# An encoder layer's expert stage: look-up order, early list rows, an early row tile and rested buffers

## The chip, the cores and the metric

The kernel runs on one core of a Trainium2 chip. The metric is the device time of one execution in microseconds (us); lower is better. The engines of the core are named as the profile names them: PE (matrix multiply, with PEld for its weight loads), DVE (vector), ACT (scalar), POOL (GpSimd, which also issues the indirect DMAs) and SP (which only issues DMAs). Each engine takes its instructions in the order in which the program put them into its queue, and an instruction that waits holds everything behind it on the same engine.

## The reference

One layer of an encoder over 256 tokens of width 2048: a retention and recurrent block, cross attention, and then PEER, a layer of 16384 single-neuron experts, ended by a normalisation. The change touches only PEER and the glue before it:

```python
def peer_ffn(xn, w_q, sub_keys, u_tab, v_tab):
    q = (xt @ w_q).reshape(t, PEER_HEADS, 2, PEER_HALF)
    sub_scores = jnp.einsum('thcd,hckd->thck', q, sub_keys)
    vals, ids = lax.top_k(sub_scores, PEER_TOPK)
    ...
    eid = (i1 * PEER_N_KEYS + i2)          # 8 heads x 16 experts a token
    gate = softmax(top_sc)
    ...
        u = u_tab[eb]
        act = gelu(einsum('td,tkd->tk', xb, u))
        return einsum('tk,tkd->td', gb * act, v_tab[eb])
```

Every token picks 128 experts. An expert costs a dot product of the token's normed row with a row of `u_tab` and the addition of a multiple of a row of `v_tab`; a row is 2048 floats, 8 KB.

## The kernel before

The kernel doesn't gather all chosen rows. It treats the experts in three ways.

- **Dense.** `RD` = 40 groups of 128 experts are computed for all tokens as matrix products: five chunks (0 to 4) of eight columns, with weights that SP loads in order (`U`, `V`).
- **Counted.** Among the other 88 groups, the 32 experts of each lane that most tokens chose are found on the chip (`choose`, `chosen_rows`) and also computed for all tokens: four chunks (5 to 8) of eight columns, whose rows are gathered by POOL with indices in `dyn`.
- **Listed.** What remains is a list for each token, `BASE` = 38 places. Tokens are lanes, in two halves `tt` of 128 tokens; place `k` of half `tt` is one gather by POOL of 128 rows (1 MB) with indices `idx[tt][:, k]`, then one DVE instruction: `dot` with a row of `Us`, later `axpy` with a row of `Vs`. The few tokens with longer lists share two `spill` operations, each with two gathers (rows of `Us`, and normed rows from `hn` in device memory).

The stages around the change, in order of time:

**The look-ups.** While PE does the last columns of the dense U chunks (`u_block`), a generator `side` is woven in: after each half column `Weave.pump` lets as much of it run as its rate allows. Before it, `gbuild` writes the gate of each expert and token to device memory (`gt<-gs`, issued by ACT); its source tiles come from the slots `qs` and `ms`, three of them in `ms`. `look_up` then finds for each token which of its experts are counted. It has eight parts, four for each half; part `i` needs one 1 MB tile of broadcast indices, loaded by `at_load(i)` on POOL into `ats[i % 6]`. The list `ats` is `h[1]`, the three `ms` tiles, and two tiles that `gbuild` uses for scratch (`gx["a"]`, `gx["d"]`). After the four parts of a half, `compact` picks its list (`pick`, `rows_of`), and after both halves it works out the spills; then the three `ms` tiles go to `ring`, the free list for gathered list rows. In this part of the program a scheduler orders the instructions; the stages after it (`manual_schedule`) are issued as written.

**The D steps.** `run` goes through a list of steps with the loads, splits and matmuls of each. A loop over `t` does, at step `t`: the transposes of step `t + 4` (`turned`), the high part of step `t + 3` on ACT (`high`), the low part of step `t + 2` on DVE (`low`), the loads for step `t + 8` (or `t + 12` for gathered rows of V and of gates), the matmuls of step `t`, and then `wv.pump(step.rate)`, which lets the generator `chosen` do list operations; one costs 2.2. The 64 D steps are the U products of the counted chunks 5 to 8, two steps to a gathered row. `chosen` refills every free buffer of `ring` with the next gather before each operation. The first half's dots use the normed rows in `h[0]`; after the last of them `hold(1)` loads the second half's rows over it, on POOL. The two spills stand between the halves.

**The V steps.** `ORDER` is the order of the chunks: 0, 1, 2, 3 (dense, 16 W steps each), then 5, 6, 7, 8 (counted, 16 R steps each), and 4 in `v_final`. Chunks 5 and 7 are `PLAIN`: their R steps run in plain float32 without a split. A counted chunk first needs its gates: a K step multiplies by 1 MB of gate rows that POOL gathers in eight parts, one at a step (`pending`). Rows of gates and of V go to the free list `rows_v`. A buffer returns to it as soon as its last reader has been issued (in `low`, or after the matmuls of a plain step). The list starts empty: when a chunk's activations are no longer needed, `given(n)` hands their tile over, to `rows_v` for `n` below 6 and to `ring` after that. The tile of chunk 0 is lent to the dense weights as two halves (`lent`) and goes to `rows_v` when the queue of W and G loads (`queues["WG"]`; G steps read dense gates) is empty.

**The end.** `v_final` does chunk 4, the last `END` = 12 axpys, the spills' second part and the final norm.

Of the kernel before, what the change touches and what calls it, by code (L numbers as in the profile page):

```python
# [18 lines left out]
P = 128  # L19
# [15 lines left out]
ND = 2  # L35
RL, RT, RN = 1.55, 2.6, 1.4
RQ = 1.3
RG, RK, RU, RV, RP = 8.0, 3.5, 2.05, 1.2, 2.0
PLAIN = (4, 5, 7)
END = 12  # L40
WARM = 18
RD = 40
RS = P - RD
# [42 lines left out]
def hybrid_layer_kernel(ctx: ExitStack, tc: tile.TileContext, a: dict, out: bass.AP, dbg=None):  # L86
# [23 lines left out]
    def slot(tag, shape, name, dt=F32):  # L110
        return b8.tile(shape, dt, tag=tag, name=name, bufs=3 if tag == "ms" else 2)
# [878 lines left out]
    def look_up(tt):  # L990
        fl = gx["b"][:, 1920:2048]
        for c in range(4):
            at = at_of(4 * tt + c)
            for n in range(0, 32, 16):
                V.tensor_scalar(at[:, n:n + 16], at[:, n:n + 16], tr["t"][:, P:], None, op0=ALU.is_equal)
                yield 0.7
            pt = sm("look")
            for n in range(32):
                PE.matmul(pt[:, NW * n:NW * n + NW], at[:, n], words, start=True, stop=True)
            if 4 * tt + c + len(ats) < 4 * TT:  # L1000
                at_load(4 * tt + c + len(ats))
            found = gx["b"][:, 512:512 + 32 * NW].rearrange("p (s w) -> p s w", w=NW)
            V.tensor_tensor(found, pt[:, :32 * NW].rearrange("p (s w) -> p s w", w=NW),
                            which[tt][:, 32 * c:32 * c + 32], op=ALU.mult)
            V.tensor_reduce(fl[:, 32 * c:32 * c + 32], found, axis=AX.X, op=ALU.add)
            yield 1.0
        fu = fl.bitcast(U32)
        V.tensor_copy(fl.bitcast(I32), fl)
        V.tensor_tensor(fu, fu, bits[tt], op=ALU.logical_shift_right)
        V.tensor_scalar(fu, fu, 31, None, op0=ALU.logical_shift_left)  # L1010
        for t in (key[tt], work[tt]):
            V.tensor_tensor(t.bitcast(U32), t.bitcast(U32), fu, op=ALU.bitwise_or)
        yield 1.0

    def compact():
        ct = pgt.tile([P, 5, TT], F32, tag="ct", name="ct")
        cnt_, more, off, end, tok = (ct[:, n] for n in range(5))
        for tt in range(TT):
            yield from look_up(tt)
            if not tt:  # L1020
                yield from chosen_rows()
            sel[tt] = tp.tile([P, NSEL], F32, tag=f"sel{tt}", name="sel")
            sel2[tt] = tp.tile([P, NSEL], F32, tag=f"gts{tt}", name="sel2")
            idx[tt] = tp.tile([P, NSEL], I32, tag=f"idx{tt}", name="idx")
            for b in range(NSEL // 8):
                pick(tt, b)
                yield 0.8
            m8 = pgt.tile([P, OVK], F32, tag="m8", name="m8")
            V.max(m8[:, :8], key[tt])
            V.tensor_scalar(more[:, tt:tt + 1], m8[:, :1], 0.0, None, op0=ALU.is_ge)  # L1030
            V.tensor_scalar(m8[:, :OVK], sel[tt][:, BASE:], 0.0, None, op0=ALU.is_ge)
            V.tensor_reduce(cnt_[:, tt:tt + 1], m8[:, :OVK], axis=AX.X, op=ALU.add)
            V.tensor_scalar(tok[:, tt:tt + 1], tr["t"][:, P:], float(tt * P), None, op0=ALU.add)
            for n, t in enumerate((key[tt], work[tt])):
                A.dma_start(spare_keys[tt, n], t)
            rows_of(tt, slice(0, NSEL))
            ov[tt] = pgt.tile([P, OVK], F32, tag=f"ov{tt}", name="ov")
            V.tensor_copy(ov[tt], idx[tt][:, BASE:])
            yield 1.4
# [44 lines left out]
                                   op0=ALU.is_equal, op1=ALU.mult, accum_out=spl["g"][:, bs])  # L1084
            yield 0.6
        count_rest()
        ring.extend(ats[1:4])

    tr = {}

    def side():
        tr["t"] = rp.tile([P, P + 1], F32, tag="cand", name="tri")
        nc.sync.dma_start(tr["t"], a["tri"])
        wv.rate = RK
        ats.extend(slot("ms", [P, D], f"at{i}") for i in (1, 2, 3))
        ats.extend((gx["a"], gx["d"]))
        for i in range(1, 6):
            at_load(i)
        yield from choose()
        yield from compact()  # L1100
# [157 lines left out]
    def v_steps(i):  # L1258
        first = i == ORDER[0]

        def products(hi, lo, dc, q):
            if not acc:
                for d in range(3):
                    acc[d] = [pz_.tile([P, 512], F32, tag="z", name=f"acc{d}{tt}") for tt in range(TT)]
                acc[3] = [mm("acc30"), mm("acc31")]
            ah, al = ahs[i]
            v_mms(ah, al, hi, lo, q, list(enumerate(acc[dc])), first)

        def column(c):
            def load(b):  # L1270
                k = 8 * (i - NCH) + c
                G.indirect_dma_start(b, None, a["Vs"], bass.IndirectOffsetOnAxis(ap=dyn[:, k:k + 1], axis=0),
                                     bounds_check=NS - 1, oob_is_err=False)
            return load

        if i in PLAIN and i >= NCH:
            for c in range(8):
                for half in range(2):
                    yield Step("R", None if half else column(c),
                               lambda row, c=c, half=half: p_mms(acts[i], row, c, half), RP, half, plain=True)  # L1280
        elif i < NCH:
            for dc in range(4):
                for q in range(4):
                    yield Step("W", lambda b, dc=dc, q=q: nc.sync.dma_start(b, a["V"][i, dc, q]),
                               lambda hi, lo, dc=dc, q=q: products(hi, lo, dc, q), RV)
        else:
            for c in range(8):
                for half in range(2):
                    yield Step("R", None if half else column(c),
                               lambda hi, lo, c=c, half=half: r_mms(*ahs[i], hi, lo, c, half), RV, half)  # L1290

    def prep_steps(i, gap=2):
        box = []
# [47 lines left out]
    def run(steps):  # L1341
        raws, his, los, pts, later = {}, {}, {}, {}, {}
        queues = {k: [t for t, s in enumerate(steps) if s.kind in k and s.load] for k in ("WG", "D", "K", "R")}
        free = {"WG": spots, "D": rows_u, "K": rows_v, "R": rows_v}

        def loads(t):
            for k, q in queues.items():
                while q and q[0] <= t + (4 if k in "KR" else 0) and free[k]:
                    t = q.pop(0)
                    raws[t] = free[k].pop(0)  # L1350
                    if k in "DR":
                        raws[t + 1] = raws[t]
                    steps[t].load(raws[t])
# [23 lines left out]
        def low(t):  # L1377
# [15 lines left out]
            if kind in "WG":  # L1393
                spots.append(raws[t])
            elif kind == "K" or kind == "R" and steps[t].part:
                rows_v.append(raws[t])
            if not queues["WG"] and lent and all(any(b is f for f in spots) for b in lent):
                spots[:] = [f for f in spots if all(b is not f for b in lent)]
                lent.clear()
                rows_v.append(held_in[ORDER[0]])  # L1400
# [8 lines left out]
        for t in range(2):  # L1409
            low(t)  # L1410
        for t, step in enumerate(steps):
            now = later.pop(t, [])
            for f, _ in now:
                if f:
# [8 lines left out]
            if step.plain:  # L1423
                step.mms(raws[t])
                if step.part:
                    rows_v.append(raws[t])
                del raws[t]
            elif step.kind not in "GK":
                step.mms(his.pop(t), los.pop(t))
# [16 lines left out]

    coef = {}

    def dot(tt, k, gat, last, k0=0):
        V.scalar_tensor_tensor(junk, gat, 1.0, h[0], op0=ALU.mult, op1=ALU.mult, accum_out=coef[tt][:, k:k + 1])  # L1450
        if k % 8 == 7 or k == last:
            s = slice(max(k - k % 8, k0), k + 1)
            A.activation(coef[tt][:, s], coef[tt][:, s], AF.Gelu_apprx_tanh)
            V.tensor_tensor(coef[tt][:, s], coef[tt][:, s], sel2[tt][:, s], op=ALU.mult)
# [20 lines left out]
    def chosen():  # L1475
        ops = []
        for tt in range(TT):
            coef[tt] = tp.tile([P, NSEL], F32, tag=f"coef{tt}", name="coef")
            for k in range(BASE):
                ops.append(("dot", tt, k, [(a["Us"], NS, idx[tt][:, k:k + 1])]))  # L1480
            if tt == 0:
                for b in range(TT):
                    ops.append(("spill", b, 0, [(a["Us"], NS, spl["i"][:, b:b + 1]), (hn, T, spl["ti"][:, b:b + 1])]))
        moves = [("axpy", tt, k, [(a["Vs"], NS, idx[tt][:, k:k + 1])]) for tt in range(TT) for k in range(BASE)]
        closing.extend(moves[-END:])
        moves = moves[:-END]
# [3 lines left out]
            moves[(n + 1) * apart] = ("pe",) + m[1:]  # L1490
        ops += moves
        gathers = [g for o in ops for g in o[3]]
        held, taken, used = [], 0, []
        for kind, tt, k, gs in ops:
            if kind in ("axpy", "pe"):
                while "hh" not in done:
# [4 lines left out]
                taken += 1  # L1501
            mine = [held.pop(0) for _ in gs]
            if kind == "dot":
                hold(tt)
                dot(tt, k, mine[0], BASE - 1)
                if tt == 0 and k == BASE - 1:
                    hold(1)
            elif kind == "spill":
                spill_dot(tt, mine[0], mine[1])
            elif kind == "axpy":  # L1510
# [244 lines left out]
        done.add("hh")  # L1755

    def given(n):
        (rows_v if n < 6 else ring).append(held_in[ORDER[n]])

    steps = [u for i in range(early, NCH + NDY) for u in u_steps(i, part if i == early else 0)]  # L1760
    attach(steps[-7], prep_steps(ORDER[0], 1)[1])
# [113 lines left out]
```

## Time and profile before

| | us |
|---|---|
| runs (3) | 1993.11 to 1997.34, median 1995.55 |
| the profiled execution's own time | 2009.42 |
| its span in the trace | 2007.6 |
| PE busy in the span | 1897.4 |
| granted TensorE clock, mean | 0.98 |

The span is what the trace covers; 1.8 us of the profiled execution's time lie around it. The profiled execution took 13.9 us longer than the median of the runs. PE is the busiest engine; in the trace its idle time stands ahead of the instruction that ended it, with what released it. Gathers are shown by what they read: `in_Us_dram,idx` and `in_Vs_dram,idx` are list rows, `in_Us_dram,dyn` and `in_Vs_dram,dyn` counted rows, `gt,dyn` gate rows, `hn,spti` and `in_Us_dram,spi` the spills'; `i1d` is what the look-ups load. `kept` is any of the nine big tiles that hold activations, scratch or, later, gathered rows, `at` a tile of `ats`, `h` one of `h[0]`, `h[1]`.

### The profile page before, as it was taken

Reading aid. Unit: us, or ns where it says so; the run is one execution under the profiler, and the core shown is the slowest. Engines: PE = TensorE matmul, PEld = TensorE weight load, DVE = VectorE, ACT = ScalarE, POOL = GpSimd, SP = SyncE. Lnnn points to the kernel's source line nnn. Section 1 sums busy time; section 2 is a strip of 40 time slices with the busy share of each in tenths; the row PEclk is TensorE's granted clock in tenths of the full one; section 3 lists DMA queues with packets and bytes.
Section 4 is the critical chain, followed back from the end, with each engine's and each line's share of the span. In section 5 each row is a group of like instructions: output and inputs, shape, how many; then the busy total and the mean of one; then the engine's idle time right before and its main releaser. Section 6 shows DMA issues by size and latency. Waiting matters only on the chain.

```text
span 2007.6 us, 28472 instructions
## 1 busy us (share of the span) xinstructions
PE 1897.4 (95%) x10644; PEld 1586.3 (79%) x10644; DVE 1498.8 (75%) x2304; ACT 851.2 (42%) x1324; POOL 521.5 (26%) x371
## 2 busy tenths in 40 slices
PE   9999999999999999999998859999899888989798
PEld 8888888888889888899998859888787767555463
DVE  6868967754566557999977647899799887676667
ACT  6566444544555545554456613333333333020211
POOL 0200010000000000000035411555433787567523
PEclk9999999999999999999999979999999989999999
DMA  8775656566664558655668895997989899979983
GB/s 298 267 226 169 203 181 194 158 189 194 184 189 141 150 182 279 183 170 180 179 159 161 182 287 157 400 393 281 376 321 392 302 373 365 362 291 379 396 350 121
DMA packets 203246, 499.92 MB, mean 249 GB/s; under 512 B 106760, under 2 KB 113032, under 8 KB 174856
## 3 DMA queue, kind: packets, MB, share of 16 engines
q1 hardware_dynamic: 72288, 254.23, 39.2%
q0 software_dynamic: 36240, 228.29, 29.5%
q10 hardware_dynamic: 94576, 15.54, 4.7%
q8 instruction: 84, 1.38, 0.3%
q14 instruction: 58, 0.48, 0.1%
HBM read 503.24 MB, written 21.30 MB: 261 GB/s over the span
## 4 chain that ended last, share of the span: by engine, by line
PE 53%; DMA 19%; DVE 14%; issue 9%; POOL 4%; ACT 1%; POOLq 0%; ACTq 0%; SPq 0%; DVEq 0%
PE wb L143 7%; PE xc L196 7%; PE xc L197 7%; PE xc L199 7%; PE U L154 6%; DMA at<-in_Us_dram,idx 4%; PE wb L145 4%; DVE lo L134 4%; PE acc L1625 3%; DMA at<-in_Vs_dram,idx 3%; DMA gt<-gs 2%; DMA h<-in_Vs_dram,idx 2%; PE G L1139 2%; POOL at L1443 2%; PE U L143 1%
## 5 line engine op out<-in xcount | busy, mean ns | idle before, releaser
L134 DVE TENSOR_TENSOR lo<-raw,hi 128x1024 fp32r<-128x1024 f32 x364 | 448.5, 1234 | 211.7 <-PE xc L199 122.3
L133 ACT CAST hi<-raw 128x1024 fp32r<-128x1024 f32 x364 | 382.2, 1053 | 363.9 <-PE xc L197 172.3
L1450 DVE SCALAR_TENSOR_TENSOR junk<-at,h 128x2048 bf16<-128x2048 f32 x72 | 164.5, 2284 | 22.8 <-DMA at<-in_Us_dram,idx 16.1
L154 PE MATMUL U<-xn,hi 128*128 128x256 f32 x1280 | 176.8, 289 | 1.5 <-ACT hi L133 1.5
L154 PEld LDWEIGHTS U<-xn,hi 128*128 128x128 f32 x1280 | 164.3, 196 | 1.7 <-ACT hi L133 1.7
L1458 DVE SCALAR_TENSOR_TENSOR hh<-at,coef,hh 128x2048 f32<-128x2048 f32 x49 | 116.0, 2367 | 57.4 <-DMA at<-in_Vs_dram,idx 56.7
L143 PE MATMUL U<-xn,hi 128*128 128x512 f32 x512 | 140.3, 407 | 0.0
L1372 ACT CAST hi<-kept 128x1024 fp32r<-128x1024 f32 x52 | 53.9, 1050 | 199.9 <-DMA kept<-in_Vs_dram,dyn 58.6
L792 POOL DMA_DIRECT2D hn<-h x2 | 1.1, 566 | 509.7 <-DVE h L790 509.7
L1443 POOL DMA_INDIRECT at<-in_Us_dram,idx x72 | 83.5, 1159 | 142.2 <-DVE junk L1450 121.3
L143 PE MATMUL wb<-hT,hi 128*128 128x512 f32 x448 | 116.9, 396 | 0.0
L1206 PE MATMUL acc<-kept,kept 128*128 128x512 f32 x256 | 110.2, 592 | 0.0
L143 PEld LDWEIGHTS U<-xn,hi 128*128 128x128 f32 x512 | 93.0, 192 | 15.4
L1126 POOL TENSOR_TENSOR kept<-kept 128x512 f32<-128x512 bf16 x64 | 72.0, 1133 | 127.3 <-DVE kept L1125 90.3
L154 PE MATMUL U<-xn,lo 128*128 128x256 f32 x640 | 93.6, 289 | 6.9 <-DVE lo L134 6.7
L1443 POOL DMA_INDIRECT at<-in_Vs_dram,idx x49 | 87.1, 1777 | 47.4 <-DVE hh L1458 20.5
L1206 PEld LDWEIGHTS acc<-kept,kept 128*128 128x128 f32 x256 | 48.6, 190 | 60.4 <-issue 60.0
L154 PEld LDWEIGHTS U<-xn,lo 128*128 128x128 f32 x640 | 84.1, 195 | 9.9 <-DVE lo L134 9.5
L143 PEld LDWEIGHTS wb<-hT,hi 128*128 128x128 f32 x448 | 80.6, 189 | 13.9
L143 PE MATMUL wb<-xT,hi 128*128 128x512 f32 x352 | 88.8, 393 | 0.0
L1125 DVE TENSOR_TENSOR kept<-kept,kept 128x512 bf16<-128x512 bf16 x128 | 63.4, 542 | 32.8 <-PE cnt L1142 21.8
L1389 DVE TENSOR_TENSOR lo<-uT,hi 128x512 fp32r<-128x512 f32 x128 | 81.8, 681 | 5.7 <-ACT hi L1370 4.6
(496 smaller groups left out, 4376.0 us busy)
## 6 DMA issues: line engine op xcount, KB each, us to landing
raw<-in_U_dram SPq DMA_DIRECT2D x80, 512.0 KB, 3.8
raw<-in_w_qkv_dram SPq DMA_DIRECT2D x48, 512.0 KB, 4.3
raw<-in_w_xyg_dram SPq DMA_DIRECT2D x44, 512.0 KB, 4.5
raw<-in_V_dram SPq DMA_DIRECT2D x44, 512.0 KB, 7.7
raw<-in_w_xk_dram SPq DMA_DIRECT2D x32, 512.0 KB, 3.7
raw<-in_w_xv_dram SPq DMA_DIRECT2D x32, 512.0 KB, 4.2
raw<-in_w_out_dram SPq DMA_DIRECT2D x32, 512.0 KB, 4.1
raw<-in_w_xq_dram SPq DMA_DIRECT2D x32, 512.0 KB, 3.7
```

Of the source, the lines that this page charges most:

```text
L133: A.copy(hi, raw)
L134: V.tensor_tensor(lo, raw, hi.bitcast(F32), op=ALU.subtract)
L143: PE.matmul(pt, hi[:, ks], xt[:, kb, :], start=(kb == 0), stop=(kb == KB - 1))
L154: PE.matmul(pt[:, :T], (lo if part == 2 else hi)[:, k * P:(k + 1) * P], x, start=(part == 0 and kb == 0), stop=(part == 2 and kb == KB - 1))
L196: PE.matmul(pt, xh, hi[:, w], start=(n == 0 and k == 0), stop=False)
L197: PE.matmul(pt, xl, hi[:, w], start=False, stop=False)
L199: PE.matmul(pt, xh, lo[:, w], start=False, stop=(n == 7 and k == 1))
L1206: PE.matmul(acc[dc][tt], av[:, c, tt * P:(tt + 1) * P], row[:, dc * 512:(dc + 1) * 512], start=False, stop=False)
L1389: V.tensor_tensor(los[t][:, s], pts[t][n], his[t][:, s].bitcast(F32), op=ALU.subtract)
L1443: G.indirect_dma_start(dst, None, src, bass.IndirectOffsetOnAxis(ap=ix, axis=0), bounds_check=n - 1, oob_is_err=False)
L1450: V.scalar_tensor_tensor(junk, gat, 1.0, h[0], op0=ALU.mult, op1=ALU.mult, accum_out=coef[tt][:, k:k + 1])
L1458: V.scalar_tensor_tensor(hh[tt], gat, coef[tt][:, k:k + 1], hh[tt], op0=ALU.mult, op1=ALU.add)
```

## The change

It has five parts.

1. **Look-up places.** `ats` becomes `h[1]`, `gx["a"]`, `gx["d"]`, then the three `ms` tiles. Parts 1 and 2 of the look-ups now use the scratch tiles of `gbuild`, parts 3, 4 and 5 the `ms` tiles, part 7 `gx["a"]`.
2. **First list rows.** The three `ms` tiles don't go to `ring` at the end. Into each, as soon as its look-up part is done and the first list is known, the gather of one of the first three places is issued (`ahead`); `chosen` starts with these three in hand.
3. **Normed rows.** During the look-ups SP loads the second half's rows from `hn` into `held_in[8]`, which is `gx["d"]`. The first `SWAP` = 8 dots of the second half read them there. After the last dot of the first half SP, not POOL, loads the same rows into `h[0]` for the others. The spills are separated: after place 19 of the first half and after place 10 of the second.
4. **Rest.** A buffer of `rows_v` goes through a list `cool` and is free again two steps later. `given` hands the tile of place 5 of `ORDER` to `ring` and no longer to `rows_v`. The lent tile returns when no W load is left in the queue, whatever G loads are.
5. **Rates.** W steps pump 1.15, no longer 1.2; the R steps that are split pump 1.3, no longer 1.2.

```diff
-RG, RK, RU, RV, RP = 8.0, 3.5, 2.05, 1.2, 2.0
+RG, RK, RU, RV, RR, RP = 8.0, 3.5, 2.05, 1.15, 1.3, 2.0
+SPILL_AT = (19, 10)
+SWAP = 8
...
+            if tt and c < 2:
+                ahead.append(fetch(ats[4 + c], a["Us"], NS, idx[0][:, 1 + c:2 + c]))
+            if tt == 0 and c == 3:
+                nc.sync.dma_start(held_in[NCH + NDY - 1], hn[P:2 * P, :])
             yield 1.0
...
             rows_of(tt, slice(0, NSEL))
+            if tt == 0:
+                ahead.append(fetch(ats[3], a["Us"], NS, idx[0][:, 0:1]))
...
         count_rest()
-        ring.extend(ats[1:4])
...
-        ats.extend(slot("ms", [P, D], f"at{i}") for i in (1, 2, 3))
         ats.extend((gx["a"], gx["d"]))
+        ats.extend(slot("ms", [P, D], f"at{i}") for i in (3, 4, 5))
...
-                               lambda hi, lo, c=c, half=half: r_mms(*ahs[i], hi, lo, c, half), RV, half)
+                               lambda hi, lo, c=c, half=half: r_mms(*ahs[i], hi, lo, c, half), RR, half)
...
+        cool, clock = [], [0]
+
         def loads(t):
+            while cool and cool[0][0] + 2 <= clock[0]:
+                rows_v.append(cool.pop(0)[1])
...
             elif kind == "K" or kind == "R" and steps[t].part:
-                rows_v.append(raws[t])
-            if not queues["WG"] and lent and all(any(b is f for f in spots) for b in lent):
+                cool.append((clock[0], raws[t]))
+            if lent and not any(steps[n].kind == "W" for n in queues["WG"]) and all(any(b is f for f in spots) for b in lent):
...
         for t, step in enumerate(steps):
+            clock[0] = t
...
                 if step.part:
-                    rows_v.append(raws[t])
+                    cool.append((t, raws[t]))
...
-    def dot(tt, k, gat, last, k0=0):
-        V.scalar_tensor_tensor(junk, gat, 1.0, h[0], op0=ALU.mult, op1=ALU.mult, accum_out=coef[tt][:, k:k + 1])
+    def dot(tt, k, gat, last, k0=0, rows=None):
+        V.scalar_tensor_tensor(junk, gat, 1.0, h[0] if rows is None else rows, op0=ALU.mult, op1=ALU.mult, accum_out=coef[tt][:, k:k + 1])
...
-            if tt == 0:
-                for b in range(TT):
-                    ops.append(("spill", b, 0, [(a["Us"], NS, spl["i"][:, b:b + 1]), (hn, T, spl["ti"][:, b:b + 1])]))
+                if k == SPILL_AT[tt]:
+                    ops.append(("spill", tt, 0, [(a["Us"], NS, spl["i"][:, tt:tt + 1]), (hn, T, spl["ti"][:, tt:tt + 1])]))
...
-        held, taken, used = [], 0, []
+        held, taken, used = list(ahead), len(ahead), []
...
-                hold(tt)
-                dot(tt, k, mine[0], BASE - 1)
+                dot(tt, k, mine[0], BASE - 1, rows=held_in[NCH + NDY - 1] if tt and k < SWAP else None)
                 if tt == 0 and k == BASE - 1:
-                    hold(1)
+                    kept_h[0] = 1
+                    nc.sync.dma_start(h[0], hn[P:2 * P, :])
...
-        (rows_v if n < 6 else ring).append(held_in[ORDER[n]])
+        (rows_v if n < 5 else ring).append(held_in[ORDER[n]])
```

More of the change, by code (lines that the diff above doesn't have):

```diff
@@ L1086, in compact @@
         count_rest()
-        ring.extend(ats[1:4])
-    tr = {}
+    tr, ahead = {}, []
     def side():
```

## The prediction

> **What bounds the kernel now.** From the page, whose span is 2007.6 us with PE busy for 95% of it, I went to a table of the stages, then to what PE waited for.
>
> ```profile
> 1247.00:1506.00 259.00, 242.88 (x1537) 214.81 (x1538) 222.88 (x288) 94.14 (x204) 128.00 (x93) 0.98 0.91 348
> 1506.00:1715.00 209.00, 185.48 (x768) 147.49 (x767) 174.37 (x139) 72.54 (x75) 136.31 (x72) 0.95 0.94 361
> 1715.00:1936.00 221.00, 202.55 (x642) 122.65 (x641) 155.03 (x86) 35.94 (x35) 125.57 (x76) 0.97 0.89 347
> ```
>
> The rows are the D steps (to 1506), the W steps (to 1715) and the R steps (to 1936); the look-ups end at 1247. Behind the length stand the busy times of PE, PEld, DVE, ACT and POOL, then granted clock, DMA share and GB/s. Behind 1936 I price nothing: the change has nothing there but more buffers for the last list rows. How long would PE alone need? The timeline has steps that follow each other without a gap:
>
> ```profile
> 1251.37 2.09 PE L143 MATMUL U<-xn,hi 128*128 128x512 f32 x8
> ...
> 1255.04 1.86 PE L143 MATMUL U<-xn,hi 128*128 128x512 f32 x7
> ```
>
> ```profile
> 1508.61 0.39 PE L1184 MATMUL acc<-hi,a 128*128 128x512 f32 x1
> ...
> 1511.33 0.39 PE L1184 MATMUL acc<-hi,a 128*128 128x512 f32 x1
> ```
>
> ```profile
> 1824.79 11.75 PE L1206 MATMUL acc<-kept,kept 128*128 128x512 f32 x27
> ```
>
> A D step takes 1255.04 - 1251.37 = 3.67 us, a W or split R step 2.72, a plain R step (8 matmuls) 8 x 11.75 / 27 = 3.48. So PE needs 64 x 3.67 = 235 us in D, 64 x 2.72 = 174 in W, 32 x 2.72 + 32 x 3.48 = 198 in R: 24, 35 and 23 less than these stages took. Some 82 us go to gaps and to the slower clock behind them. Who makes the gaps stands in PE's list of waits (total, times, longest):
>
> ```profile
> PE acc L1187 <- DVE lo L1392: 18.6, 8, 8.6
> PE uT L1361 <- DVE lo L1389: 15.8, 9, 6.7
> PE acc L1200 <- DVE lo L1392: 15.5, 4, 10.3
> ```
>
> In the large ones it is DVE, which is not short of time (223 of 259 us busy in D): its queue stands at an instruction whose gather or load hasn't landed. PE is the bound, and a gap is a transfer that came late.
>
> **The change part by part.** The terms go against the profiled execution, 2009.42 us.
>
> *Look-up places.* The timeline of POOL and of PE:
>
> ```profile
> 1157.95 0.58 POOL L988 DMA_DIRECT2D kept<-i1d  x1 [0.30 <-POOL kept L1126]
> ...
> 1193.23 0.57 POOL L988 DMA_DIRECT2D at<-i1d  x1 [22.96 <-DMA gt<-gs]
> ```
>
> ```profile
> 1199.65 0.59 PE L999 MATMUL look<-words,at 128*128 128x11 bf16 x16 [14.92 <-DVE at L995]
> 1200.10 0.60 PE L999 MATMUL look<-words,kept 128*128 128x11 bf16 x17
> ...
> 1212.48 2.08 PE L154 MATMUL U<-xn,hi 128*128 128x256 f32 x16
> ...
> 1215.36 2.08 PE L154 MATMUL U<-xn,hi 128*128 128x256 f32 x16
> ```
>
> The last `ms` tile is free only when the last gate write (`gt<-gs`) has landed, at 1192.7; its index load went out at 1193.23 and PE stood 14.92 us for it. The scratch tiles' loads had gone out from 1157.95. The change doesn't take the write away: it gives that tile to part 5 instead of part 3. Parts 0 to 4 and the first half's picks can then run in the wait, but PE still has a part that needs this tile. Where will that part stand among the U half columns (1215.36 - 1212.48 = 2.88 us each)? By the generator's yields part 5 comes 13.6 credits, or 4 half columns at `RK` = 3.5, behind part 3; 4 x 2.88 = 11.5 us of PE work would fill most of the gap. But the second row shows a `kept` part (4) beside part 3: the order went by when data were thought ready, not by the place in the program. The tile is ready as late as before, so I take **0**. The bounds: -15 (the gap goes) to +14 (the picks stand before the splits on DVE, and the five half columns that PE did ahead of the gap, 5 x 2.88, come behind it). The early load of `hn`, 1 MB, 3.0 us at 348 GB/s, may delay that write by as much, within these bounds.
>
> *First list rows.*
>
> ```profile
> 1261.59 1.97 PE L1361 MATMUL uT<-ident,row 128*128 128x128 f32 x8 [3.52 <-DVE lo L1389]
> ```
>
> ```profile
> at<-in_Us_dram,idx POOLq DMA_INDIRECT x72, 8.5
> ```
>
> Today the first gathers are issued as the D steps begin and land 8.5 us later; DVE stands at the first dot, PE runs out of low parts and loses 3.52 us. With three rows in place, the gather that refills the first buffer has three dots' time, 3 x 3.67 x 2.2 / 2.05 = 11.8 us, to land. The same number of gathers and dots is done: **-4** with the slow matmuls behind the gap (1.97 for eight transposes). Three gathers, 3.1 MB, leave a stretch that the next rows show full; bounds -8 to 0.
>
> *Spills and the reload of `h[0]`.*
>
> ```profile
> 1416.65 1.32 PE L1361 MATMUL uT<-ident,h 128*128 128x128 f32 x8 [2.19 <-DVE lo L1389]
> ...
> 1427.42 1.97 PE L1361 MATMUL uT<-ident,h 128*128 128x128 f32 x8 [6.66 <-DVE lo L1389]
> ```
>
> ```profile
> 1250.00:1375.00 125.00, 119.19 (x760) 105.28 (x759) 109.64 (x142) 44.15 (x99) 67.85 (x49) 0.99 0.98 382
> 1375.00:1430.00 55.00, 46.12 (x291) 41.05 (x290) 42.35 (x54) 17.18 (x40) 27.55 (x21) 0.96 0.81 301
> 1430.00:1506.00 76.00, 74.60 (x464) 65.50 (x463) 69.28 (x92) 30.59 (x62) 31.87 (x25) 0.99 0.90 341
> ```
>
> A spill takes two of three buffers. The first cost PE 2.19 us, the second, with no lead left, 6.66. Apart, each should cost what the first did: 2 x 2.19 against 8.85 is -4.5, and with less slow clock **-5**; bounds -10 (both hidden) to +5 (both like the second). The reload moves from POOL to SP, so no gather stands behind its wait for the last dot; the early copy covers dots 0 to 7. But SP waits instead, and behind it stand the first four loads of V:
>
> ```profile
> 1233.17 5.95 SPq L1284 DMA_DIRECT2D raw<-in_V_dram  x4
> ```
>
> They went out ahead of the D steps. Now 2.1 MB, 5.5 us at 382 GB/s, come after the reload, in stretches with 0.19 x 55 + 0.10 x 76 = 18 us of free transfer time: **+1**, up to +5.5 if that cover fails. They are first read at step 64, long after.
>
> *Rate of the W steps.* 64 x 0.05 / 2.2 = 1.5 list operations fewer, each a DVE instruction of some 2.3 us. The big gaps there are K steps:
>
> ```profile
> 1624.86 2.29 DVE L1306 TENSOR_TENSOR kept<-kept,kept 128x2048 f32<-128x2048 f32 x1 [7.50 <-DMA kept<-gt,dyn]
> ```
>
> The gate rows' issue steps don't change (a count through `run` gives the same steps), so these gaps stay: **-3**, bounds -7 to +4. The 1.5 operations come back in the split R steps, beside 66 us in which DVE is idle: 0, or +3.5 uncovered.
>
> *Rest and buffers.* POOL's waits and, for one place, the timelines:
>
> ```profile
> POOL kept L1272 <- DVE lo L1392: 24.9, 7, 7.3
> POOL kept L1272 <- PE acc L1206: 15.5, 8, 3.6
> ```
>
> ```profile
> 1882.32 2.86 POOL L1272 DMA_INDIRECT kept<-in_Vs_dram,dyn  x1 [5.51 <-DVE lo L1392]
> ...
> 1892.29 0.99 POOL L1443 DMA_INDIRECT h<-in_Vs_dram,idx  x1 [0.30 <-issue]
> ```
>
> ```profile
> 1905.28 2.35 DVE L1458 SCALAR_TENSOR_TENSOR hh<-h,coef,hh 128x2048 f32<-128x2048 f32 x1 [9.25 <-DMA h<-in_Vs_dram,idx]
> ```
>
> POOL stood 40 us at counted rows whose buffer still had a reader. Such a wait holds back every list gather behind it: 5.51 us at 1882, so the gather of 1892.29 came late, DVE stood 9.25 us at its axpy, and PE had its longest gap, 10.3. Rested buffers have no reader left, and from chunk 6 on the list has five buffers instead of four. What is late next is the transfers themselves (DMA share 0.89). Of the 10.3 and some 2 us of slow clock I take -8, of the other 15.5 - 10.3 = 5.2 us -3: **-11**, bounds -20 to 0.
>
> Sum: 0 - 4 - 5 + 1 - 3 + 0 - 11 = **-22**: 1987.4 in a profiled execution, which was 13.9 us above the median of the runs. Forecast: 1995.55 - 22 = **1973.5**.
>
> **The rivals.**
> - *The look-up gap goes too.* Part 5 keeps its four half columns: -11.5 and about -1.5 of slow clock, sum -35: **1960.5**. For it: the first half's list no longer hangs on the last write. Against: the `kept` row.
> - *Transfers bound the stages.* Waits go, but 0.91, 0.94 and 0.89 of DMA are used already, so gaps move: -4 for the first rows, -2 for the spills, -3 for the rest: **1986.5**. A sharper form: if 348, 361 and 347 GB/s were all that can be had, only moved bytes count, 3.1 MB out and 2.1 MB into D, 1 MB / 348 = -3: 1992.6. The Trainium skill ("DMA: Bandwidth & Descriptors", Specifications) states some 358 GB/s as the memory's limit for a core, by which the sum would be this -3. The trace disagrees: 382 over 125 us.
> - *Slower: rested rows come late.* With five row buffers in split R steps a row comes round every 10 steps, 27.2 us; it must be there three steps early, is freed one step before its second half and rests two: 4 steps, which leaves 6, 16.3 us, for POOL and the transfer. Landing of counted rows:
>
> ```profile
> DMA to landing us min/median/max: 6.7/10.1/17.0
> ```
>
>   With today's worst POOL wait, 7.3, it is 17.4 already. From 16.3 on each row is late; 2 us on each of 16 rows is +32, sum +10: **2005.5**. Against: the rest removes just those waits.
> - *The parts do nothing* (other waits take over everywhere): within 4 us of **1995.5**.
>
> **How the numbers follow.** The forecast 0.47, the look-up gap 0.22, transfers 0.20 (0.03 of it at 1992.6), late rows 0.07, nothing 0.04. 0.2% is 4 us, about what a measurement of this kernel can tell. Below 1991.6 lie the forecast, the gap and most of transfers: faster 0.84. Same: 0.08. Slower: late rows and a bad end of the look-ups (+14 with small gains elsewhere), 0.08. The range goes from 1950 (the gap rival with the better ends of its terms) to 1992.
>
> **What would show it.** Look-ups: one wait of 10 us or more of PE at L999, now behind the first half's `pick`; its absence means the first rival. First rows: no gap of PE at the first D steps. Spills: two L1531 waits apart, each with at most 2 us of PE. Rest: POOL at L1272 waits for DVE or PE less than 10 us in all, and no gap of PE above 5 us behind 1860. I am wrong if R's length doesn't fall, if DVE's waits for list rows stay as long, or if the U columns end over 5 us later.

## The result, and the profile after

| | before | after |
|---|---|---|
| runs, median (5 each) | 1997.34 us (1993.11 to 2003.56) | 1978.31 us (1977.11 to 1982.86) |
| ratio | | 0.9904, 95% interval 0.988 to 0.9929 |
| profiled execution, span | 2007.6 us | 1977.0 us |

The change takes 1% off, 19 us. The forecast was 1973.5 us, 22 less than the median known then. To see whether it was right for the reasons given, cut each trace where the first matmul of a stage starts:

| us | ahead | look-ups | D | W | R | end |
|---|---|---|---|---|---|---|
| before, first trace | 1015.7 | 231.3 | 258.9 | 209.5 | 221.0 | 71.2 |
| before, second trace | 1017.4 | 232.8 | 253.7 | 203.8 | 220.5 | 71.2 |
| after | 1019.7 | 233.7 | 254.4 | 196.8 | 198.5 | 73.9 |

The second trace of before (run `before_again` below) is there because the first execution was some 12 us longer than the median. Most of that excess stood in D and W; R is the same in both. So what the change did to D and W is read against several traces, and R can be read from one.

The three stages of after in windows; the columns are those of the prediction (length, busy PE, PEld, DVE, ACT, POOL, granted clock, DMA share, GB/s):

```profile
1253.00:1508.00 255.00, 241.71 (x1537) 215.47 (x1538) 223.24 (x289) 95.21 (x205) 124.70 (x89) 0.98 0.91 350
1508.00:1705.00 197.00, 182.62 (x769) 146.05 (x768) 172.12 (x137) 72.74 (x76) 122.51 (x70) 0.97 0.96 371
1705.00:1903.00 198.00, 197.16 (x640) 120.10 (x639) 153.65 (x87) 35.39 (x35) 135.56 (x79) 1.00 0.98 393
```

In the last row PE is busy for 197.16 of 198 us, at the full clock: the R steps now run at the pace that the prediction worked out for PE alone (198). Of the 22.5 us that R lost, 202.55 - 197.16 = 5.4 are matmuls that no longer run at a low clock behind a gap (the mean granted clock of R was 0.97 and is 1.00); the rest is idle time of PE. W lost gaps too, D hardly. What PE waits for in the whole of after (total, times, longest):

```profile
PE uT L1372 <- DVE lo L1400: 12.7, 6, 4.3
PE acc L1194 <- DVE lo L1403: 10.3, 7, 6.9
...
PE look L1001 <- DVE at L997: 8.0, 1, 8.0
...
PE acc L1207 <- DVE lo L1403: 0.3, 1, 0.3
```

The last line is the split R steps: 15.5 us before, 0.3 now. The first is the D steps: 15.8 before, 12.7 now. The timeline of PE says where these waits stand:

```profile
1205.75 0.59 PE L1001 MATMUL look<-words,at 128*128 128x11 bf16 x16 [8.05 <-DVE at L997]
...
1253.39 3.71 PE L1372 MATMUL uT<-ident,row 128*128 128x128 f32 x32 [0.47 <-ACT kept L1179]
...
1346.06 1.31 PE L1372 MATMUL uT<-ident,row 128*128 128x128 f32 x8 [3.25 <-DVE lo L1400]
...
1444.23 1.97 PE L1372 MATMUL uT<-ident,h 128*128 128x128 f32 x8 [3.29 <-DVE lo L1400]
...
1475.73 1.97 PE L1372 MATMUL uT<-ident,h 128*128 128x128 f32 x8 [4.32 <-DVE lo L1400]
...
1628.75 2.07 PE L1194 MATMUL acc<-lo,xe 128*128 128x512 f32 x4 [6.92 <-DVE lo L1403]
```

The first row is the last look-up tile, the second the start of D, where the gap of 3.52 us is gone. The rows at 1346 and 1475 are the two spills, the one at 1628 the K step of chunk 6 (K6 from here on, and so for the others). The one at 1444 is new, and SP shows why:

```profile
1414.68 0.33 SPq L1518 DMA_DIRECT2D h<-hn  x1
1415.10 2.77 SPq L1291 DMA_DIRECT2D raw<-in_V_dram  x4
```

SP waited for the last dot of the first half, then issued the reload and, behind it, the four loads of V, 3.1 MB issued within 3.2 us, while the list needs its own rows. From 1415 to 1450 the DMA engines then have a share of 1.01, at 405 GB/s. POOL's waits at the counted rows in after:

```profile
POOL kept L1279 <- DVE lo L1403: 16.9, 5, 15.7
POOL kept L1279 <- PE acc L1213: 7.6, 4, 3.1
```

They sum to 24.5 us, 15.7 of them one wait ahead of R, against 40.4 before; the prediction had named less than 10 in all as its sign. DVE's waits for list rows of V, whose length was another sign, fell from 88.3 to 57.0 us. A third one, U columns that end over 5 us later, did show: D starts at 1253.4, 6.4 us later than in the first trace of before and 3.2 later than in the second. Of the 6.4 us, 4.0 stand ahead of the look-ups.

### The profile page after: what moved, and what is told of

It reads as the page before. It is cut to its first block, busy times and chain, and to the rows that moved or that the text cites. A ratio compares the mean times of both kernels' runs of the same rounds, so it can differ in the third digit from the quotient of the medians.

```text
span 1977.0 us, 28501 instructions
## 1 busy us (share of the span) xinstructions
PE 1896.1 (96%) x10644; PEld 1589.4 (80%) x10644; DVE 1500.9 (76%) x2304; ACT 851.6 (43%) x1324; POOL 517.7 (26%) x370
## 4 chain that ended last, share of the span: by engine, by line
PE 56%; DMA 17%; DVE 14%; issue 9%; POOL 2%; ACT 2%; ACTq 0%; SPq 0%; POOLq 0%; DVEq 0%
PE wb L145 8%; PE xc L198 7%; PE xc L199 7%; PE xc L201 7%; DMA at<-in_Us_dram,idx 6%; PE acc L1213 6%; PE wb L147 4%; PE U L156 4%; DVE lo L136 4%; DMA gt<-gs 3%; DMA at<-in_Vs_dram,idx 2%; DMA kept<-in_V_dram 2%; PE G L1146 2%; PE acc L1194 2%; PE acc L1191 2%
## 5 line engine op out<-in xcount | busy, mean ns | idle before, releaser
L1462 DVE SCALAR_TENSOR_TENSOR junk<-at,h 128x2048 bf16<-128x2048 f32 x64 | 146.2, 2284 | 9.1 <-DMA at<-in_Us_dram,idx 8.9
L1470 DVE SCALAR_TENSOR_TENSOR hh<-at,coef,hh 128x2048 f32<-128x2048 f32 x46 | 108.0, 2348 | 47.3 <-DMA at<-in_Vs_dram,idx 46.7
L1455 POOL DMA_INDIRECT at<-in_Vs_dram,idx x46 | 76.0, 1653 | 41.0 <-issue 18.6
```

The lines of the kernel that those rows point to most:

```text
L1455: G.indirect_dma_start(dst, None, src, bass.IndirectOffsetOnAxis(ap=ix, axis=0), bounds_check=n - 1, oob_is_err=False)
L1462: V.scalar_tensor_tensor(junk, gat, 1.0, h[0] if rows is None else rows, op0=ALU.mult, op1=ALU.mult, accum_out=coef[tt][:, k:k + 1])
L1470: V.scalar_tensor_tensor(hh[tt], gat, coef[tt][:, k:k + 1], hh[tt], op0=ALU.mult, op1=ALU.add)
```

## The experiments

Times are medians; each ratio is to runs of the kernel before on the same chip. Stages are cut as above.

**The parts by themselves.** Four kernels, the first of them before itself, for a second trace (one run, 2001.21 us):

```diff
before_again: unchanged
part4_only: the kernel before with part 4 of the change alone (rest, hand-over, lent tile)
rates_only: the kernel before with part 5 alone
-RG, RK, RU, RV, RP = 8.0, 3.5, 2.05, 1.2, 2.0
+RG, RK, RU, RV, RR, RP = 8.0, 3.5, 2.05, 1.15, 1.3, 2.0
...
parts123: the changed kernel without parts 4 and 5
```

> The kernel before, unchanged, for a second trace. Its first trace was 12 us above its median and lost 24, 35 and 23 us in the D, W and R stages. If those gaps belong to the kernel, the second trace loses them within some 5 us a stage and has PE gaps of 6 us or more at the second spill (D) and of 8 or more near the end of R. Rival: part of the first trace's loss was that execution's own; then W or R is 10 us or more shorter here.

> The kernel before with part 4 alone (rest of two steps, tile of place 5 to the list, lent tile back early). My theory: the R stage falls by 11 us or more (in the changed kernel's trace it fell by 22), POOL's waits at L1272's counterpart fall from 40 us to under 10, the W stage stays within 4 us, so 0.989 to 0.995 of the time before. Rival: the R stage is ended by transfers and gains only with the thinner W pace of part 5 as well; then 0.997 or above.

> The kernel before with part 5 alone (W steps pump 1.15, split R steps 1.3). My theory: W 3 us shorter, R as long or up to 3.5 longer: 0.998 to 1.001. Rival: the pace made the whole of the changed kernel's shorter W stage (-12.7 us in the traces): 0.993 to 0.996.

> The changed kernel with parts 4 and 5 undone: look-up order, early list rows, early normed rows, spills apart, reload on SP. My theory: D 8 us shorter, look-ups within 3 us: 0.994 to 0.998. Rival: what the D stage gains is lost again at the next gap (in the changed kernel's trace D fell by only 4.5 us); then 0.998 to 1.001 with the W stage no shorter than before.

| | time, us | ratio, 95% | look-ups | D | W | R | end |
|---|---|---|---|---|---|---|---|
| part4_only | 1980.06 | 0.9895 (0.9864 to 0.9925) | 232.7 | 254.3 | 201.4 | 197.0 | 71.1 |
| rates_only | 1987.47 | 0.9928 (0.99 to 0.9955) | 229.1 | 256.8 | 197.1 | 214.8 | 71.1 |
| parts123 | 2005.13 | 1.0008 (0.9986 to 1.0029) | 235.6 | 255.6 | 209.7 | 217.9 | 71.1 |

`before_again` has its gaps where they were expected, 7.29 us at the second spill and 10.8 near the end of R; D and W moved by 5.2 and 5.7 us, a little more than the 5 that its theory allowed.

Part 4 alone brings R to PE's own pace:

```profile
1706.00:1903.00 197.00, 197.00 (x642) 120.77 (x641) 155.31 (x87) 36.12 (x35) 130.08 (x77) 1.00 0.99 399
```

The time came out as its theory said. POOL's waits did not: they were to fall under 10 us, and 31.4 are left, 14.1 of them one wait ahead of R. PE doesn't notice the 17.3 in R:

```profile
POOL kept L1272 <- DVE lo L1396: 15.8, 6, 14.1
POOL kept L1272 <- PE acc L1206: 15.6, 8, 3.6
```

The rates alone shorten W, which the forecast gave 3 us, and R, which it gave none; the whole, 0.9928, is the rival's and not the theory's:

```profile
1502.00:1699.00 197.00, 180.75 (x770) 144.00 (x769) 171.81 (x138) 72.58 (x75) 124.82 (x71) 0.98 0.97 374
1699.00:1914.00 215.00, 203.37 (x643) 124.04 (x642) 158.17 (x88) 35.98 (x35) 128.90 (x77) 0.97 0.93 368
```

Parts 1 to 3, which the forecast gave 8 us, change nothing that can be measured, as the rival had it: the look-ups, the first rows, the spills and the reload together.

**One step of the changed kernel put back.** Four kernels, and the diff of each against after:

```diff
after_no_rest
-            while cool and cool[0][0] + 2 <= clock[0]:
+            while cool and cool[0][0] <= clock[0]:
...
after_rows6
-        (rows_v if n < 5 else ring).append(held_in[ORDER[n]])
+        (rows_v if n < 6 else ring).append(held_in[ORDER[n]])
...
part45: parts 1 to 3 put back as before
after_pool_reload
-                    kept_h[0] = 1
-                    nc.sync.dma_start(h[0], hn[P:2 * P, :])
+                    hold(1)
```

> The changed kernel with the rest of two steps taken out; the lent tile's early return and the fifth list buffer stay. My theory: POOL's waits at a buffer's last reader make the R stage's gaps, so they return (40 us of waits at L1272's counterpart), R is 210 us or longer instead of 198.5, and the whole is 0.995 or more of the time before. Rival: the fifth list buffer does it; then R stays under 203 and the whole at 0.992 or less.

> The changed kernel with the tile of place 5 going to the row buffers as before (six rows, four list buffers); rest and the lent tile's early return stay. My theory (the rest does it): R under 203 us, 0.992 or less. Rival (the fifth list buffer does it): R 210 or longer, 0.995 or more.

> The kernel before with parts 4 and 5 and without 1 to 3. My theory: parts 1 to 3 gave nothing (1.0008 alone), so this is as fast as the changed kernel or faster: W 197, R 198, look-ups and D as before, the end some 3 us longer than before since list operations move to the end; 0.985 to 0.990. Rival: parts 1 to 3 help once R is short, because the list is then further ahead; then 0.992 or more.

> The changed kernel with the reload of h[0] issued by POOL again. My theory: the first four V loads are out of the D stage again (issued about 1240), the gap of 3.3 us behind the reload (at 1444 in the changed kernel's trace) goes, D is 3 us shorter, about 251; 0.988 to 0.990. Rival: POOL's wait for the last dot holds the list gathers back by as much; D stays at 254 or more.

| | time, us | ratio, 95% | look-ups | D | W | R | end |
|---|---|---|---|---|---|---|---|
| after_no_rest | 1979.31 | 0.9866 (0.9849 to 0.9882) | 231.5 | 257.2 | 196.3 | 205.8 | 71.1 |
| after_rows6 | 1977.47 | 0.9864 (0.9844 to 0.9884) | 232.8 | 252.7 | 197.4 | 199.5 | 71.0 |
| part45 | 1976.7 | 0.9854 (0.9838 to 0.9871) | 231.8 | 256.0 | 197.8 | 198.2 | 73.6 |
| after_pool_reload | 1969.89 | 0.9822 (0.9803 to 0.984) | 233.2 | 250.5 | 197.4 | 198.4 | 74.0 |

The rest was the heart of the forecast's largest term. Without it POOL's waits at counted rows are back:

```profile
POOL kept L1279 <- DVE lo L1403: 27.9, 7, 15.6
POOL kept L1279 <- PE acc L1213: 19.2, 12, 3.2
```

Of these 47.1 us, 15.6 are the one wait ahead of R that after has too; 31.5 stand in R, against 24.5 - 15.7 = 8.8 in after and 40.4 before. Most of the waits are back, yet R is 205.8 and not 221, and the whole kernel no slower against before than the changed one (0.9866, 0.9904). R thus lies between theory (210 or longer) and rival (under 203), and the whole is the rival's: removing these waits can't have been worth 22 us. `after_rows6` and `part45` came out as their theories had it; by `part45` (0.9854), the kernel loses nothing without parts 1 to 3. And the reload back on POOL makes the changed kernel clearly better: V's loads go out ahead of D again,

```profile
1234.76 9.04 SPq L1291 DMA_DIRECT2D raw<-in_V_dram  x4
```

and PE's waits in D fall from 12.7 to 9.2 us, with no gap of a microsecond between 1366 and 1469; the one that stood at 1444 is gone:

```profile
PE uT L1372 <- DVE lo L1400: 9.2, 5, 3.8
```

On the same chip this kernel takes 1969.89 us and `part45`, which lacks parts 1 to 3, 1976.7. So parts 1 to 3 without the reload on SP are worth 6.8 us, which with the reload on SP is gone (`parts123`: 1.0008).

**What in part 4 shortens R.** With the rest cleared of most of it, two pieces were left: the lent tile that comes back early, and the tile that goes to the list. Each was put alone into the kernel before:

```diff
lent_only
-            if not queues["WG"] and lent and all(any(b is f for f in spots) for b in lent):
+            if lent and not any(steps[n].kind == "W" for n in queues["WG"]) and all(any(b is f for f in spots) for b in lent):
...
fifth_only
-        (rows_v if n < 6 else ring).append(held_in[ORDER[n]])
+        (rows_v if n < 5 else ring).append(held_in[ORDER[n]])
```

> The kernel before with one line of part 4 alone: the lent tile goes back when no W load is left in the queue, so chunk 5 has its fourth row buffer from its start; no rest, no fifth list buffer, old rates. Theory (the early fourth buffer is a good part of what R gained, since after_no_rest kept it and lost only 7 us): R falls from about 220.7 to 205-211 us, the other stages stay as before, ratio 0.992 to 0.996. Rival (the tile helps only together with the rest or the rates): R stays at 217 or more, ratio 0.998 or more.

> The kernel before with the other hand-over alone: the tile of place 5 goes to the list and no longer to the rows. Theory (it matters only where there are row buffers to spare): R within 3 us of 220.7, ratio 0.998 to 1.002. Rival (list gathers were what came late in R, and a fifth list buffer gives them lead): R at 212 or less, ratio 0.996 or less.

| | time, us | ratio, 95% | look-ups | D | W | R | end |
|---|---|---|---|---|---|---|---|
| lent_only | 1988.59 | 0.9928 (0.99 to 0.9956) | 231.0 | 254.7 | 202.6 | 207.0 | 71.2 |
| fifth_only | 1988.65 | 0.9928 (0.9897 to 0.9959) | 229.5 | 256.7 | 203.7 | 202.2 | 72.3 |

`lent_only` did what was expected of it. `fifth_only` did not: taken out of the changed kernel the tile seemed worth 1 us of R (`after_rows6`), put alone into the kernel before it takes 18.6 off. Its R steps, and POOL's waits at the counted rows in them:

```profile
1707.00:1909.00 202.00, 198.68 (x641) 120.00 (x640) 151.17 (x85) 35.41 (x35) 131.39 (x76) 1.00 0.95 376
```

```profile
POOL kept L1272 <- PE acc L1206: 25.6, 12, 4.4
POOL kept L1272 <- DVE lo L1392: 12.8, 5, 6.6
```

POOL waits 38.4 us, as it did before, and PE hardly stands. How can the same wait cost 10 us in one kernel and nothing in the other? The place that made the longest gap of before (POOL 5.51 us at 1882, the gather of 1892.29, DVE 9.25 us at its axpy) has a counterpart in `fifth_only`, in the timelines of POOL and of DVE:

```profile
1865.82 0.99 POOL L1272 DMA_INDIRECT kept<-in_Vs_dram,dyn  x1 [3.94 <-DVE lo L1392]
...
1869.63 1.97 POOL L1272 DMA_INDIRECT kept<-in_Vs_dram,dyn  x1 [0.30 <-issue]
1871.91 1.96 POOL L1272 DMA_INDIRECT kept<-in_Vs_dram,dyn  x1 [0.30 <-issue]
1874.17 1.97 POOL L1443 DMA_INDIRECT h<-in_Vs_dram,idx  x1 [0.30 <-issue]
```

```profile
1876.33 2.35 DVE L1458 SCALAR_TENSOR_TENSOR hh<-at,coef,hh 128x2048 f32<-128x2048 f32 x1
1879.72 2.35 DVE L1458 SCALAR_TENSOR_TENSOR hh<-at,coef,hh 128x2048 f32<-128x2048 f32 x1
1885.99 2.35 DVE L1458 SCALAR_TENSOR_TENSOR hh<-h,coef,hh 128x2048 f32<-128x2048 f32 x1 [0.52 <-DMA h<-in_Vs_dram,idx]
```

POOL stands at a counted row, three counted rows and a list row go out, then the list gather into `h` at 1874.17, as before. It lands no sooner: 11.8 us later, against 13.0. But DVE has two axpys in hand whose rows are there, and comes to this one when it has landed: 0.52 us. In before it had one, and then stood:

```profile
1892.55 2.35 DVE L1458 SCALAR_TENSOR_TENSOR hh<-at,coef,hh 128x2048 f32<-128x2048 f32 x1 [0.30 <-DMA at<-in_Vs_dram,idx]
```

One more list buffer is that lead.

A fifth buffer isn't the only way past this gap. `lent_only` has four, and POOL waits as long in its R steps as before, 28.6 + 26.1 - 14.3 (one wait ahead of R) = 40.4 us:

```profile
POOL kept L1272 <- DVE lo L1392: 28.6, 6, 14.3
POOL kept L1272 <- PE acc L1206: 26.1, 11, 6.1
```

```profile
1868.35 2.86 POOL L1272 DMA_INDIRECT kept<-in_Vs_dram,dyn  x1 [4.22 <-DVE lo L1392]
1871.52 1.97 POOL L1272 DMA_INDIRECT kept<-in_Vs_dram,dyn  x1 [0.30 <-issue]
1873.79 1.96 POOL L1443 DMA_INDIRECT h<-in_Vs_dram,idx  x1 [0.30 <-issue]
```

```profile
1883.15 2.35 DVE L1458 SCALAR_TENSOR_TENSOR hh<-h,coef,hh 128x2048 f32<-128x2048 f32 x1 [1.47 <-DMA h<-in_Vs_dram,idx]
```

Behind the wait two counted rows go out and then the gather into `h`, 5.4 us after the wait's end and not 10.0, and DVE stands 1.47 us in place of 9.25. So the row can be made to land in time as well by fewer rows ahead of it.

**Versions that might beat both.** Two kernels, from after_pool_reload:

```diff
reload_rows6
-        (rows_v if n < 5 else ring).append(held_in[ORDER[n]])
+        (rows_v if n < 6 else ring).append(held_in[ORDER[n]])
...
reload_rows6_k: reload_rows6, and
-                while q and q[0] <= t + (4 if k in "KR" else 0) and free[k]:
+                while q and q[0] <= t + {"K": 7, "R": 4}.get(k, 0) and free[k]:
```

> The changed kernel with two things put back: the reload of h[0] on POOL (no load of V waits for it) and the tile of place 5 to the rows. Theory (both gains are apart from each other: the reload shortens D to about 251, the tile takes the 2.8 us from the end and costs R one): D about 251, R about 199.5, end about 71; ratio 0.980 to 0.983, 2 to 3 us better than after_pool_reload. Rival (end and R only trade): 0.983 or more, no better than after_pool_reload.

> reload_rows6 with the gate rows of a K step allowed to start 15 instead of 12 steps ahead (by count K6 starts 13 ahead, K7 and K8 15, K5 still 12). Theory (the W gap that is left, 6.9 us at K6, is the gate rows' transfer coming late): that gap falls to about 4 or less, W 2 to 4 us shorter than the 197 of the other kernels with the new rates, ratio 0.978 to 0.982. Rival (earlier gate rows only push back the list gathers on POOL): the gap moves to another step, W within 1.5 us of 197, ratio as reload_rows6 or worse.

| | time, us | ratio, 95% | look-ups | D | W | R | end |
|---|---|---|---|---|---|---|---|
| reload_rows6 | 1969.29 | 0.9831 (0.9803 to 0.9858) | 233.5 | 251.2 | 196.2 | 198.7 | 71.1 |
| reload_rows6_k | 1973.39 | 0.985 (0.9819 to 0.9881) | 234.4 | 252.1 | 197.9 | 198.8 | 71.1 |

In the first, every stage came out as the theory had it, the end 2.9 us shorter than in after_pool_reload, but the runs show no gain, as the rival had it: 1969.29 against 1969.89, on two chips, and a ratio of 0.9831. In the second the gap at K6 falls and another stands behind it, at K7, as the rival said:

```profile
1623.10 1.22 PE L1194 MATMUL acc<-lo,xe 128*128 128x512 f32 x2 [4.02 <-DVE lo L1403]
...
1648.44 1.97 PE L1194 MATMUL acc<-lo,xe 128*128 128x512 f32 x4 [3.60 <-DVE lo L1403]
```

4.02 + 3.60 us, where reload_rows6 had one gap of 7.12. Ahead of the second, DVE stands 3.8 us for a list row. The best kernels are thus after_pool_reload and reload_rows6, 1.7 to 1.8% under before.

## Why the prediction came out right, step by step

The sum was right (-22 forecast, -19 in the runs) because errors in its terms cancelled; that the total came out is luck. What held is the place of the largest gain, R, and the chain that leads to its gaps. Against the mean of all traces with and without the part in question:

| term | forecast | runs showed |
|---|---|---|
| look-up places | 0 | +2.3 (233.5 over 7 traces with parts 1 to 3, 231.2 over 7 without) |
| first rows, spills, V loads behind SP | -4 - 5 + 1 = -8 | D -0.9 (255.0 over 4 traces, 255.9 over 7) |
| W rate | -3 | -8 (197.1 over 8 traces, 205.1 over 6) |
| R rate, rest and buffers | 0 - 11 | -22.3 (198.5, 220.8 over 2 traces) |
| end | not priced | +2.7 |

The right column sums to -26, as the spans of the traces do (2003.5 in the mean, 1977.0 after). The runs gave -19: both traces of before come from executions above the 1997.34 of the result. Which terms hold the 7 us too many is open. It is least likely R's, whose two traces agree to half a microsecond.

*Look-up places.* Right in place, and within the bounds in size. POOL still issues the last tile's index load when the last gate write has landed:

```profile
1199.85 0.53 POOL L990 DMA_DIRECT2D at<-i1d  x1 [19.09 <-DMA gt<-gs]
```

PE then waits 8.05 us, where 10 or more was named, but behind the first half's `pick`, as said. The second trace of before has the stand in two parts, 9.13 and 7.68 us. So the gap did shrink, and yet the stage is 2.3 us longer; only part of what took the gap's place is known (PE stands 3.4 us more for `words`, before the first look-up). The rival in which the gap goes gave a shorter stage.

*First rows.* The gap at the first D steps is gone, as said. It doesn't show in D's length, since the loads behind the reload cost about as much (below).

*Spills.* The step that failed is "each should cost what the first did: 2 x 2.19". Apart, they cost 3.25 and 4.32 us in after, 3.08 and 3.78 in after_pool_reload; together 7 to 7.6, against 8.85 in the first trace of before and 7.29 in the second, all of it at the second spill. So at most 1 to 2 us in place of 5; the sign, at most 2 us each, did not come. A spill takes two gathers for one operation, wherever it stands.

*V loads behind SP.* The step that failed is "**+1**", with the argument that free transfer time covers them: "They are first read at step 64, long after." They are not late themselves; the list rows beside them are. With the reload on POOL and these loads ahead of D, D takes 250.5, 251.2 and 252.1 in three kernels, 251.3 in the mean, against 255.0: +3.7, within the bound of 5.5 that was given and not taken. Putting the reload back moves its own issue as well as that of the four loads; that it is the loads is read from the full DMA share there and was not separated by a run. The early copy of `hn`, the three early rows and the spills apart then are worth 255.9 - 251.3 = 4.6 together, in the traces.

*W rate.* The term was too small, but by how much is open. The -8 is a mean over kernels with and without part 4. With part 4 in, the rates take W from 201.4 (`part4_only`) to 197.8 (`part45`), 3.6 us, near the forecast; without it, from 206.7 (before, two traces) to 197.1 (`rates_only`), 9.6. The gaps at the K steps, said to stay, shrank in part: in rates_only K6 stands for 7.01 us, 8.55 before. The step that failed is that only the 1.5 operations' own time comes off. In before, DVE also stands for list rows in W:

```profile
DVE hh L1458 <- DMA h<-in_Vs_dram,idx: 7.1, 2, 4.1
DVE hh L1458 <- DMA at<-in_Vs_dram,idx: 6.5, 3, 2.9
```

These are 13.6 us, and 7.8 to 13.1 in the other five traces with the old rates. With the new rates there is no such wait in W in seven of the eight traces; the eighth is reload_rows6_k with its 3.8. One gap of before's PE that follows such waits, 5.61 us at 1692, is gone too. So at the slower pace the list's rows land in time. That R, too, lost 6 us in rates_only was not foreseen and isn't explained.

*Rest and buffers.* The chain was read rightly in its last links: a list gather is late, DVE stands, PE has its gap. Nearly all the idle time of R went with it, 221.0 - 202.6 = 18.4 us, and 5.4 of slow clock, where the forecast took 11 of the two. It held back because "What is late next is the transfers themselves"; they weren't: with a DMA share of 0.98 and 393 GB/s PE stands for 0.84 us. The step that failed is "Rested buffers have no reader left" as the one cure, for 40 us of POOL's waits. `fifth_only` leaves 38.4 us of these waits and has 18.6 of the 22 us; `lent_only` leaves 40.4 and has 13.8; `after_no_rest` has 31.5 us of them in R and still 15. So the waits' length doesn't set the price. Where the traces were read place by place, what counted was the lead of the list, for which the prediction had half a sentence, "the list has five buffers instead of four". Put alone into the kernel before, the tile for the list is worth 18.6 us of R, the early lent tile 13.8, the rates 6.0; taken out of the changed kernel, the rest is worth 7.3, the tile 1.0. These don't add up, since PE's own pace is a floor, and one piece gains what another would; nor is more always better: the tile alone (202.2) stands lower than tile, lent tile and rates together without the rest (205.8). So part 4 as a whole is shown to be the cause, and a split of the 22 us among its pieces can't be given. What the early lent tile does for the list was read at one place only, and neither the rest alone in the kernel before nor the rest with the old return of the lent tile was tried.

*End.* "Behind 1936 I price nothing" was an omission. The three kernels with the list's fifth buffer, the new rates and the rest end in 73.6 to 74.0 us, `fifth_only` in 72.3, all others in 71.0 to 71.2. It is worth little: `reload_rows6` is rid of it and runs no faster than `after_pool_reload`.

*The rivals.* "Transfers bound the stages" falls: R moves its bytes at 393 to 399 GB/s where it had 347. "Rested rows come late" falls: PE waits 0.3 us in split R steps.

## What to carry to other kernels

A wait at the head of an in-order queue costs little while the engine that it starves has work in hand (38.4 us of POOL's waits left PE 3.3 of 202 us idle in `fifth_only`); ask for the lead of the starved engine (how many rows are there when the queue stops), and price the gap by that, not by the length of the wait. Where several cures aim at one bound, each can look worth nearly all of the gain alone and nothing when taken out of the whole, so test both ways. And an instruction that is moved to another queue takes what is behind it along: here one reload on SP moved 2.1 MB of loads into a stretch where the DMA engines were full, and with them went most of what the step had won (3.7 of 4.6 us of D).

## What the runs showed of the hardware that was not expected

The 347 GB/s of R's steps were no limit of the transfers: the DMA engines had a share of 0.89 there before, and moved 399 GB/s over 197 us in `part4_only` at a share of 0.99, with PE never standing. The Trainium skill ("Perfetto Trace Analysis", Engine Utilization) says that a single active core can draw more than the 358 GB/s per core, up to what its 16 DMA engines carry, about 435; the measured 399 / 0.99 = 403 GB/s agrees with the first and stays below the second.

Two executions of the same kernel, before, differ by 8.2 us of span: the second is 5.7 shorter in W and 5.2 in D and 3.2 longer ahead of D, while R differs by half a microsecond. A single trace can thus misplace a gain of this size between stages; the terms for D and W above rest on means for that reason.
